# Six tiles wide at the start, squares on ScalarE, zero-padded rotary keys, and the samples' products in one run

## The chip, the core and the metric

The kernel runs on one core of a Trainium2 chip. TensorE (PE) multiplies matrices, VectorE (DVE) and ScalarE (ACT) work element by element, GpSimd (POOL) does the same more slowly and issues transfers, and SyncE (SP) issues most of the transfers. Each engine works through its own instructions in order and waits on semaphores for the others. The metric is the device time of one launch in microseconds (us), median of three runs.

## What is computed

One step of one layer for 256 prompt tokens and 8 samples of 16 tokens each, so 384 columns of tokens (`T`), with a model width of 2048. The layer has a group of eight latent-attention heads, a group of four gated-linear-attention heads (keys of 128, values of 256), an output projection, a gated feed-forward part and an embedding gate. What matters here:

```python
a = rms_norm(h, g_pre_mix)
z = a @ w_in                      # q-latent, kv-latent, rotary key, GLA q, k, v, gate, output gate
# latent attention, per head
s = einsum('bqhc,bkc->bhqk', q_lat, ckv) + einsum('bqhr,bkr->bhqk', q_rope, kr)   # kr: 64 wide, one for all heads
# gated linear attention of the samples: one block of 16 tokens, state S0 (8 samples, 4 heads, 128, 256)
attn = einsum('bthd,btshd,bshd->bhts', qf, decay, kf)
o  = einsum('bhts,bshv->bthv', attn, vf) + einsum('bthd,bhdv->bthv', qf * exp(b), S0)
S1 = exp(b_last)[..., None] * S0 + einsum('bshd,bshv->bhdv', kf * exp(b_last[:, None] - b), vf)
```

All inputs and outputs are float32.

## The kernel before, in words

**Products.** Large products run at float32 accuracy out of three faster ones. A weight chunk arrives in `raw`; ACT casts it to a high part `wh` (L89) and DVE subtracts to get the low part `wl` (L90); activations are split the same way (`ah`, `al`, L113 and L114). `mm3` (L98 to L101) then issues three matmuls per tile: high by high, high by low, low by high, over 384 columns. In names of the trace the tile written stands left of the arrow. Small products are plain float32 matmuls, of which one shows as two records in the trace.

**The start.** Eight matmuls on zeros (`warm`, L122) come first. `gemm_group` computes the four tiles of the GLA queries (`qg`), for 16 k-steps of 128 rows, with 12 matmuls per step in the first steps. For each k-step `load_x` loads a slice of x (SP, L274), makes its high and low parts, squares it on POOL (L280 for the first, L283 for the other 15) and adds the square to `ssx` on DVE (L284). `ssx` gives the norm's factor `rx` through `col_sums` (tile `sx`, L147). The banks are evicted with `rx` (L309). After it come the `misc` tile (rotary key and gate, L99 to L101 on 80 rows), four key tiles `kg` one by one (`win_tile`), then the statistic `pr` (L336).

**The samples' stage.** It is interleaved with the products `ckv` and `uq`, whose matmuls fill PE. For each half of the samples (four samples): the keys are transposed (`pk`, L574) and placed (`ks`, L577 and L579), the values are moved by POOL's transfers (`vs`, L585). Two output banks are opened by a matmul of zeros over the whole bank (L591), the scores' products of 32 columns add to them (L595, 16 per half, into four groups of 32 rows), and then, head by head, two states are loaded (POOL, L603) and four products of 16 columns with them (L606). The new states take a product (`pst`, L612), an update on DVE (L615) and a store (POOL, L617). Tiles come from a ring of ten buffers with the tag `tmp`. POOL also subtracts two low parts of the mixer's input there (`mixl`, L109).

**The prompt's scores.** The attention loop goes over four pairs of heads. For each head and each block of queries (128 and 256 columns wide) one product with the latent keys (nope, L703, contraction 128) is followed by one with the rotary keys (L704): the two heads of a pair lie in rows 0 to 63 and 64 to 127 of `cqn`, and the rotary keys stand twice in `krd`, so the contraction is over 64 rows.

**What sets the order.** The program is written in stages, and a scheduler that simulates the engines puts each engine's instructions in order by priorities; `tc.high_priority` moves loads and splits ahead, `tc.issue_after` holds a transfer behind an instruction. The order is fixed when the program is built.

Of the kernel before, what the change touches and what calls it, by code (L numbers as in the profile page):

```python
# [56 lines left out]
def layer(ctx: ExitStack, tc: tile.TileContext, I, O):  # L57
# [12 lines left out]
    PIECES = ((1, 1, 1, 1), (2, 2), (2, 2), (4,))  # L70
# [53 lines left out]
    with tc.high_priority(offset=2 * PRIO):  # L124
        sp.dma_start(out=gains, in_=I["gains"])
# [52 lines left out]
    def gemm_wide(srcs, a, name):  # L178

        banks = [bank(f"{name}{n}", "g" if n < 4 else "s") for n in range(WIDE)]  # L180
        cols = WIDE * P
        for c in range(NK // 2):
            pieces = (1, 1) if c == 0 else (2,)
            raw = stream.tile([P, 2048], F32, name="raw", tag="raw")
            k0 = 2 * c
            for n in pieces:
                with tc.high_priority(offset=PRIO):
                    at_k = (k0 - 2 * c) * cols
                    piece = raw[:, at_k:at_k + n * cols]
                    sp.dma_start(out=piece, in_=srcs[c][:, at_k:at_k + n * cols])  # L190
                    subs = split(piece, n * cols, cols)
                for k in range(n):
                    for m in range(WIDE):
                        mm3(banks[m][:, :T], at(subs[k], slice(None), slice(m * P, m * P + P)), a(k0 + k),
                            k0 + k == 0, k0 + k == NK - 1)
                k0 += n
        return [b[:, :T] for b in banks]

    def gemm_group(srcs, a, name, before=None):

        banks = [bank(f"{name}{n}") for n in range(4)]
        k0 = 0
        for c in range(4):
            pieces = PIECES[c] if before else PIECES[0 if c == 0 else 3]
            if len(pieces) > 1:
                raw = stream.tile([P, 2048], F32, name="raw", tag="raw")
            for i, n in enumerate(pieces):
                if before:
                    before(k0, n)
                if len(pieces) > 1:  # L210
                    with tc.high_priority(offset=PRIO):
                        at_k = sum(pieces[:i])
                        piece = raw[:, at_k * 512:(at_k + n) * 512]
                        sp.dma_start(out=piece, in_=srcs[c][:, at_k * 512:(at_k + n) * 512])
                        subs = split(piece, n * 512)
                else:
                    subs = weights(srcs[c])
                order = [(k, m) for k in range(n) for m in range(4)]
                if c == 3:
                    order = [(k, m) for m in range(4) for k in range(n)]  # L220
                for k, m in order:
                    w = subs[k // 2]
                    col = (k % 2) * 512 + m * P
                    kk = k0 + k
                    mm3(banks[m][:, :T], at(w, slice(None), slice(col, col + P)), a(kk), kk == 0, kk == NK - 1)
                k0 += n
        return [b[:, :T] for b in banks]
# [64 lines left out]
    win = iter(range(29))  # L292
# [35 lines left out]
    for h in range(GH):  # L328
        ps = win_tile("kg")
        for c in range(3):  # L330
            sl = slice(c * P, (c + 1) * P)
            dve.tensor_tensor(out=kg[c][:, h, :], in0=ps[:, sl], in1=rx[:, sl], op=ALU.mult)
# [216 lines left out]
    with tc.high_priority(offset=AHEAD):  # L549
# [12 lines left out]
        zero = gla.tile([P, 512], F32R, name="zero", tag="tmp", bufs=NTMP)  # L562
        pool.memset(zero.bitcast(F32), 0.0)
        for half in range(2):
# [23 lines left out]

            po = [bank("o", "s") for _ in range(2)]
            for o in po:  # L590
                pe.matmul(o, lhsT=zero[:, :P], rhs=zero, start=True, stop=False)  # L591
            for h in range(GH):
                for j in range(4):
                    col = h * P + (4 * half + j) * LB
                    pe.matmul(po[h // 2][32 * j:32 * j + 32, h % 2 * DV:(h % 2 + 1) * DV], lhsT=ats[:, col:col + 32],  # L595
                              rhs=vt[:, 2, h * DV:(h + 1) * DV], start=False, stop=False)
            for h in range(GH):
                s0 = []
                for i in range(2):
                    b = 4 * half + 2 * i  # L600
                    s0.append(gla.tile([P, 2, DV], F32, name="s0", tag="tmp", bufs=NTMP))
                    with tc.high_priority(offset=400), tc.issue_after(last_sq[-1].ins):
                        pool.dma_start(out=s0[i], in_=I["state"][b:b + 2, h].rearrange("b d v -> d b v"))  # L603
                for j in range(4):
                    b = 4 * half + j
                    pe.matmul(po[h // 2][32 * j:32 * j + LB, h % 2 * DV:(h % 2 + 1) * DV],  # L606
                              lhsT=qe[:, h, b * LB:(b + 1) * LB], rhs=s0[j // 2][:, j % 2], start=False, stop=h % 2 == 1)
                for i in range(2):
# [5 lines left out]
                    for e in range(2):  # L614
                        dve.scalar_tensor_tensor(out=s0[i][:, e], in0=s0[i][:, e], scalar=ebs[:, h, b + e:b + e + 1],  # L615
                                                 in1=pst[:, e * DV:(e + 1) * DV], op0=ALU.mult, op1=ALU.add)
                    pool.dma_start(out=O["gla_s"][b:b + 2, h].rearrange("b d v -> d b v"), in_=s0[i])  # L617
# [49 lines left out]

    smask = cst[:, C_SM:C_SM + 3 * P]
    for hp in range(4):
# [28 lines left out]
        for n in range(2):  # L698
            h = 2 * hp + n
            rows = slice(64 * n, 64 * n + 64)  # L700
# [432 lines left out]
```

## Time and profile before

| what | value |
|---|---|
| three runs | 1902.71, 1901.04, 1902.37 us |
| median | 1902.37 us |
| the profiled execution, its own time | 1902.81 us |
| its span, first to last instruction | 1901.0 us |
| busy: PE | 1883.6 us (99%) |
| busy: DVE, ACT, POOL | 974.7, 690.2, 80.4 us |
| mean granted clock of TensorE | 0.998 |

The span is 1.8 us shorter than that execution's own time; this lies around it. PE is the busiest engine by far, and the chain of work that ended last runs along it for 78% of the span. Busy means that an instruction is under way: it doesn't tell whether that instruction runs at its best rate. This is read from the distance between the starts of neighbouring matmuls in the timeline.

### The profile page before, as it was taken

What the parts mean: (1) busy time and instruction counts of PE and PEld (TensorE: products, weight loads), DVE (VectorE), ACT (ScalarE), POOL (GpSimd) and SP (SyncE); (2) the same over time, 40 slices, a digit from 0 to 9 for tenths busy, and PEclk for the clock granted to TensorE, in tenths of its full rate; (3) what the DMA queues carried; (4) which work ended last, traced back from release to release, by engine and by line L of the source; (5) the groups of instructions that cost most, each with busy time, mean ns of one, the idle gap of its engine ahead of it and who ended that gap; (6) DMA issues with size and microseconds to landing.
All of it is one profiled execution on the core that took longest, in us unless ns stands there. A gap on an engine that the chain in (4) does not pass through costs nothing.

```text
span 1901.0 us, 24107 instructions
## 1 busy us (share of the span) xinstructions
PE 1883.6 (99%) x10026; PEld 1709.8 (90%) x10026; DVE 974.7 (51%) x1368; ACT 690.2 (36%) x1044; POOL 80.4 (4%) x122
## 2 busy tenths in 40 slices
PE   8999999999999999999999999999999999999998
PEld 8989998788999988889988998899888988899998
DVE  7445756754233395445334643554355435456753
ACT  4344545643233453333333222322232222325432
POOL 4000002411000000000000000000000000000010
PEclk9999999999999999999999999999999999999999
DMA  6333325635743333343333333333333333334351
GB/s 239 136 110 112 112 89 176 213 138 204 258 169 133 130 122 133 111 136 130 133 133 123 122 133 133 129 118 130 133 133 111 133 133 133 111 111 147 128 177 67
DMA packets 43311, 262.53 MB, mean 138 GB/s; under 512 B 5441, under 2 KB 6481, under 8 KB 17090
## 3 DMA queue, kind: packets, MB, share of 16 engines
q1 hardware_dynamic: 36018, 233.76, 35.7%
q0 software_dynamic: 7184, 27.23, 4.1%
q8 instruction: 78, 1.28, 0.3%
q14 instruction: 31, 0.25, 0.0%
HBM read 251.17 MB, written 8.75 MB: 137 GB/s over the span
## 4 chain that ended last, share of the span: by engine, by line
PE 78%; DVE 1%; ACT 0%; issue 0%; DVEq 0%; ACTq 0%
PE gu L896 12%; PE gu L897 12%; PE gu L895 12%; PE dn L101 6%; PE dn L100 6%; PE dn L99 6%; PE mix L101 2%; PE pg L99 2%; PE pg L101 2%; PE pg L100 2%; PE mix L99 2%; PE mix L100 2%; PE psc L774 2%; PE pol L800 2%; PE ps L704 0%; DVE zT L957 0%
## 5 line engine op out<-in xcount | busy, mean ns | idle before, releaser
L90 DVE TENSOR_TENSOR wl<-raw,wh 128x1024 fp32r<-128x1024 f32 (+2 forms) x426 | 512.0, 1203 | 652.5 <-ACT wh L89 651.5
L89 ACT CAST wh<-raw 128x1024 fp32r<-128x1024 f32 (+2 forms) x426 | 435.8, 1023 | 980.5 <-PE gu L897 448.8
L896 PE MATMUL gu<-wl,fh 128*128 128x512 f32 x1056 | 411.5, 390 | 0.1
L897 PE MATMUL gu<-wh,fl 128*128 128x512 f32 x1056 | 409.2, 389 | 0.0
L895 PE MATMUL gu<-wh,fh 128*128 128x512 f32 x1056 | 406.9, 389 | 0.1
L896 PEld LDWEIGHTS gu<-wl,fh 128*128 128x128 f32 x1056 | 198.2, 188 | 42.7 <-DVE wl L90 1.7
L895 PEld LDWEIGHTS gu<-wh,fh 128*128 128x128 f32 x1056 | 198.2, 188 | 41.3 <-ACT fh L113 0.4
L897 PEld LDWEIGHTS gu<-wh,fl 128*128 128x128 f32 x1056 | 198.2, 188 | 41.0
L99 PE MATMUL dn<-sh,wh 128*128 128x384 f32 x704 | 235.1, 334 | 0.0
L100 PE MATMUL dn<-sl,wh 128*128 128x384 f32 x704 | 235.1, 334 | 0.0
L101 PE MATMUL dn<-sh,wl 128*128 128x384 f32 x704 | 234.7, 335 | 0.0
L101 PEld LDWEIGHTS dn<-sh,wl 128*128 128x128 f32 x704 | 132.0, 188 | 1.3 <-DVE wl L90 1.3
L99 PEld LDWEIGHTS dn<-sh,wh 128*128 128x128 f32 x704 | 132.1, 188 | 0.2
L100 PEld LDWEIGHTS dn<-sl,wh 128*128 128x128 f32 x704 | 132.1, 188 | 0.2
L957 DVE STREAM_TRANSPOSE zT<-z 32x384 f32<-32x384 f32 x176 | 100.3, 570 | 2.8
L984 DVE TENSOR_TENSOR acc<-acc,dn 128x384 f32<-128x384 f32 x80 | 44.3, 553 | 99.2 <-PE dn L101 98.8
L99 PE MATMUL mix<-mixh,wh 128*128 128x384 f32 x256 | 85.6, 334 | 0.0
L101 PE MATMUL pg<-h2h,wl 128*128 128x384 f32 x256 | 85.5, 334 | 0.0
L100 PE MATMUL pg<-h2l,wh 128*128 128x384 f32 x256 | 85.5, 334 | 0.0
L100 PE MATMUL mix<-mixl,wh 128*128 128x384 f32 x256 | 85.5, 334 | 0.0
L101 PE MATMUL mix<-mixh,wl 128*128 128x384 f32 x256 | 85.5, 334 | 0.0
L99 PE MATMUL pg<-h2h,wh 128*128 128x384 f32 x256 | 82.6, 334 | 0.0
(358 smaller groups left out, 2417.9 us busy)
## 6 DMA issues: line engine op xcount, KB each, us to landing
raw<-in_wgu SPq DMA_DIRECT2D x87, 1024.0 KB, 4.8
raw<-in_wd SPq DMA_DIRECT2D x40, 1024.0 KB, 4.8
raw<-in_win SPq DMA_DIRECT2D x20, 1024.0 KB, 4.9
raw<-in_wout SPq DMA_DIRECT2D x16, 1024.0 KB, 4.8
raw<-in_wpg SPq DMA_DIRECT2D x10, 1024.0 KB, 4.8
raw<-in_wvg SPq DMA_DIRECT2D x8, 1024.0 KB, 4.9
keys<-in_ckT POOLq DMA_DIRECT2D x8, 1024.0 KB, 5.6
raw<-in_ck SPq DMA_DIRECT2D x8, 1024.0 KB, 5.0
```

Of the source, the lines that this page charges most:

```text
L89: act.copy(out=h[:, :n], in_=raw[:, c:c + n])
L90: dve.tensor_tensor(out=l[:, :n], in0=raw[:, c:c + n], in1=h.bitcast(F32)[:, :n], op=ALU.subtract)
L99: pe.matmul(out, lhsT=w[0], rhs=a[0], start=start, stop=False)
L100: pe.matmul(out, lhsT=w[0], rhs=a[1], start=False, stop=False)
L101: pe.matmul(out, lhsT=w[1], rhs=a[0], start=False, stop=stop)
L774: pe.matmul(ps[:, :HK], lhsT=q.rearrange("p h t -> p (h t)"), rhs=keys[:, j, i * HK:(i + 1) * HK], start=j == 0, stop=j == 4)
L800: pe.matmul(o, lhsT=vals[:, k, j * P:(j + 1) * P], rhs=pT[:, k], start=k == 0, stop=False)
L895: pe.matmul(out[c], lhsT=ah, rhs=w[0], start=k == 0, stop=False)
L896: pe.matmul(out[c], lhsT=ah, rhs=w[1], start=False, stop=False)
L897: pe.matmul(out[c], lhsT=al, rhs=w[0], start=False, stop=k == NK - 1)
L957: dve.transpose(out=dst[cols, :, :, rows], in_=src[rows, :, :, cols])
L984: dve.tensor_tensor(out=acc[:, n], in0=acc[:, n], in1=ps, op=ALU.add)
```

## The change

Four parts:

- The first group is six tiles wide: `gemm_wide` computes four `qg` and two `kg` tiles together (tile `qk`), from a weight laid out by k-steps (`wqk`), 18 matmuls per step. The first weight piece is loaded as 256 and 512 columns. `gemm_group` and `PIECES` go. The squares of x are ScalarE activations, the gains are loaded from ACT's queue, and the constants and the statistic come at k = 14.
- The samples' scores are copied to a zeroed tile `aw` of 128 columns per head; four full products per half open the banks, and the zero products and the 32-wide products go.
- All eight states of a half are loaded first; the products with them then stand in one run, from the last head to the first; the updates follow in that order.
- The rotary keys are copied to `krz`, once with rows 64 to 127 zero and once with rows 0 to 63 zero, so the rotary product contracts over 128 rows of `cqn`.

```diff
-    def gemm_wide(srcs, a, name):
+    def gemm_wide(srcs, a, name, before=None):
...
-            pieces = (1, 1) if c == 0 else (2,)
+            pieces = (1, 1) if c < (2 if before else 1) else (2,)
...
+                if before:
+                    before(k0, n)
...
+                    parts = ((0, 2 * P), (2 * P, cols)) if before and k0 == 0 else ((0, n * cols),)
+                    for lo, hi in parts:
+                        piece = raw[:, at_k + lo:at_k + hi]
+                        sp.dma_start(out=piece, in_=srcs[c][:, at_k + lo:at_k + hi])
+                        subs += [(w, lo % cols) for w in split(piece, hi - lo, cols)]
...
-        sp.dma_start(out=gains, in_=I["gains"])
+        act.dma_start(out=gains, in_=I["gains"])
...
-                pool.tensor_tensor(out=ssx, in0=xk, in1=xk, op=ALU.mult)
+                act.activation(out=ssx, in_=xk, func=AF.Square)
...
-                last_sq.append(pool.tensor_tensor(out=sq, in0=xk, in1=xk, op=ALU.mult))
+                last_sq.append(act.activation(out=sq, in_=xk, func=AF.Square))
...
-        if k0 == 12:
+        if k0 == 14:
...
-    for h, ps in enumerate(gemm_group(I["wqg"], a, "qg", load_x)):
+    for h, ps in enumerate(gemm_wide(I["wqk"], a, "qk", load_x)):
+        if h >= GH:
+            keys(h - GH, ps)
+            continue
...
-            for o in po:
-                pe.matmul(o, lhsT=zero[:, :P], rhs=zero, start=True, stop=False)
+            aw = tmp(gla)
+            pool.memset(aw, 0.0)
+            act.copy(out=aw.rearrange("p (h j t) -> p h j t", h=GH, j=4)[:, :, :, :LB],
+                     in_=at_[2][:, :, 64 * half:64 * half + 64].rearrange("p h (j t) -> p h j t", j=4))
             for h in range(GH):
-                for j in range(4):
-                    col = h * P + (4 * half + j) * LB
-                    pe.matmul(po[h // 2][32 * j:32 * j + 32, h % 2 * DV:(h % 2 + 1) * DV], lhsT=ats[:, col:col + 32],
-                              rhs=vt[:, 2, h * DV:(h + 1) * DV], start=False, stop=False)
+                pe.matmul(po[h // 2][:, h % 2 * DV:(h % 2 + 1) * DV], lhsT=aw[:, h * P:(h + 1) * P],
+                          rhs=vt[:, 2, h * DV:(h + 1) * DV], start=h % 2 == 0, stop=False)
...
+            for h in reversed(range(GH)):
+                for j in (3, 2, 1, 0):
                     b = 4 * half + j
                     pe.matmul(po[h // 2][32 * j:32 * j + LB, h % 2 * DV:(h % 2 + 1) * DV],
-                              lhsT=qe[:, h, b * LB:(b + 1) * LB], rhs=s0[j // 2][:, j % 2], start=False, stop=h % 2 == 1)
+                              lhsT=qe[:, h, b * LB:(b + 1) * LB], rhs=s0[h][j // 2][:, j % 2], start=False, stop=h % 2 == 0)
...
+    krz = of[:, 8:10]
+    pool.memset(krz, 0.0)
+    for e in range(2):
+        rows = slice(64 * e, 64 * e + 64)
+        act.copy(out=krz[rows, e], in_=krd[rows, :TP])
...
-                pe.matmul(o, lhsT=cqn[rows, hp, qt], rhs=krd[rows, kt], start=False, stop=True)
+                pe.matmul(o, lhsT=cqn[:, hp, qt], rhs=krz[:, n, kt], start=False, stop=True)
```

How the order of instructions moves. The first place is ACT at the start. `ah` is the high part of a slice of x, `wh` that of a weight piece. Before:

```order
L116 ACT_TABLE_LOAD
L113 ACTIVATE ah_99<-x,gains 128x384
L89 CAST wh<-raw 128x512
L113 ACTIVATE ah_99<-x,gains 128x384
L89 CAST wh<-raw 128x512
```

Now, where `ssx<-x` and `ev<-x` are squares:

```order
L124 DMA gains<-in_gains 128x74
L115 ACT_TABLE_LOAD
L257 ACTIVATE ssx<-x 128x384
L112 ACTIVATE ah_99<-x,gains 128x384
L88 CAST wh<-raw 128x256
L88 CAST wh<-raw 128x512
L112 ACTIVATE ah_99<-x,gains 128x384
L260 ACTIVATE ev<-x 128x384
L88 CAST wh<-raw 128x768
```

The gains' issue and the squares have come to ACT, and the casts are of 256 and 512 columns at first, then of 768.

The second place is PE in the first half of the samples' stage. `o` is the samples' output bank, `s_` with a number a state tile, `ckv` the product between which it stands. Before:

```order
L101 MATMUL ckv<-ah_101,wl 128x384
L591 MATMUL o<-zero 128x512
L595 MATMUL o<-vt,atts 32x256 x3
L591 MATMUL o<-zero 128x512
L595 MATMUL o<-vt,atts 32x256 x13
L606 MATMUL o<-s_2929,qeb 16x256 x2
L606 MATMUL o<-s_2931,qeb 16x256 x2
L606 MATMUL o<-s_2949,qeb 16x256 x2
L606 MATMUL o<-s_2951,qeb 16x256 x2
L606 MATMUL o<-s_2969,qeb 16x256 x2
L606 MATMUL o<-s_2971,qeb 16x256 x2
L99 MATMUL ckv<-ah_101,wh 128x384
```

Now, where `tmp` in `o<-vt,tmp` is the padded score tile `aw`:

```order
L98 MATMUL ckv<-ah_101,wh 128x384
L590 MATMUL o<-s_2937,qeb 16x256
L576 MATMUL o<-vt,tmp 128x256 x2
L590 MATMUL o<-s_2937,qeb 16x256
L590 MATMUL o<-s_2935,qeb 16x256 x2
L590 MATMUL o<-s_2933,qeb 16x256 x2
L590 MATMUL o<-s_2931,qeb 16x256 x2
L99 MATMUL ckv<-al_102,wh 128x384
```

The run is now of eight state products and starts with a later load; the other eight of the half (two heads) stand together 36 products further on, where two pairs stood alone before.

The third place is POOL in the second half of that stage, where loads of states, stores of new states and the two subtractions `mixl` share one queue. Now:

```order
L584 DMA s_3080<-in_state 128x2x256
L584 DMA s_3082<-in_state 128x2x256
L602 DMA out_gla_s<-s_2937 128x2x256
L602 DMA out_gla_s<-s_2931 128x2x256
L108 ISA
L108 TENSOR_TENSOR mixl_3282<-og,mixh_3281 128x8x128
L602 DMA out_gla_s<-s_2933 128x2x256
L584 DMA s_3084<-in_state 128x2x256
L584 DMA s_3086<-in_state 128x2x256
L108 TENSOR_TENSOR mixl_3282<-og,mixh_3281 128x8x128
```

Before, a load stood ahead of each of the two subtractions and the third and fourth load behind both; now two loads stand ahead, two between them, and the instruction `ISA` (POOL's library) has come from the first square to here. On PE at the prompt's scores of the first pair of heads, `ps` before:

```order
L703 MATMUL ps<-kv,qn 128x128
L704 MATMUL ps<-krd,cqn 128x128
L703 MATMUL ps<-kv,qn 128x256
L704 MATMUL ps<-krd,cqn 128x256
L703 MATMUL ps<-kv,qn 128x128
L704 MATMUL ps<-krd,cqn 128x128
L703 MATMUL ps<-kv,qn 128x256
L704 MATMUL ps<-krd,cqn 128x256
```

Now, behind 40 products since the two nope products of 128 columns (`of` holds the padded keys):

```order
L695 MATMUL ps<-of,cqn 128x128
L694 MATMUL ps<-kv,qn 128x256
L695 MATMUL ps<-of,cqn 128x256
L695 MATMUL ps<-of,cqn 128x128
L694 MATMUL ps<-kv,qn 128x256
L695 MATMUL ps<-of,cqn 128x256
```

The rotary product takes the padded keys, and in this pair the first two nope products stand ahead of the rest.

## Rows read from the trace of the kernel before

**Rows 1.** The page's first part: busy time, share and instructions of each engine.

```profile
PE 1883.6 (99%) x10026; PEld 1709.8 (90%) x10026; DVE 974.7 (51%) x1368; ACT 690.2 (36%) x1044; POOL 80.4 (4%) x122
```

**Rows 2.** Waits of PE: engine and line, waited for, total us, times, longest.

```profile
PE qg L101 <- DVE wl L90: 2.6, 2, 2.3
PE pk L574 <- DVE s L615: 2.4, 1, 2.4
PE pv L692 <- ACT kv L685: 1.5, 1, 1.5
```

**Rows 3.** Timeline of PE, start: start us, us, operation, count, idle before and releaser.

```profile
6.28 0.69 PE L99 MATMUL qg<-ah,wh 128*128 128x384 f32 x1 [1.04 <-ACT wh L89]
...
10.29 1.02 PE L99 MATMUL qg<-ah,wh 128*128 128x384 f32 x3
...
37.11 0.44 PE L101 MATMUL qg<-ah,wl 128*128 128x384 f32 x1 [2.34 <-DVE wl L90]
...
47.81 0.34 PE L99 MATMUL misc<-ah,wh 128*80 128x384 f32 x1
...
56.18 0.33 PE L99 MATMUL kg<-ah,wh 128*128 128x384 f32 x1
```

**Rows 4.** Windows: us, busy of PE, PEld, DVE, ACT, POOL, clock, DMA share, GB/s.

```profile
20.00:30.00 10.00, 9.89 (x57) 9.57 (x57) 10.00 (x13) 4.15 (x6) 5.75 (x4) 1.00 0.77 302
```

**Rows 5.** Groups by line and shape: count, busy us, mean ns, idle before.

```profile
L114 DVE SCALAR_TENSOR_TENSOR al<-x,gains,ah 128x384 fp32r<-128x384 f32 x16 | 13.7, 878 | 2.6 <-ACT ah L113 2.6
...
L114 DVE SCALAR_TENSOR_TENSOR fl<-hh,gains,fh 128x384 fp32r<-128x384 f32 x16 | 9.8, 614 | 0.2 <-ACT fh L113 0.2
...
L90 DVE TENSOR_TENSOR wl<-raw,wh 128x768 fp32r<-128x768 f32 x16 | 15.3, 956 | 10.1 <-ACT wh L89 10.0
...
L89 ACT CAST wh<-raw 128x768 fp32r<-128x768 f32 x16 | 13.4, 836 | 17.8 <-PE pg L100 14.1 <-issue 3.3 <-PE ple L100 0.4
```

**Rows 6.** Timeline of PE in the samples' stage, both halves.

```profile
308.16 0.40 PE L591 MATMUL o<-zero 128*128 128x512 f32 x1
...
311.02 1.67 PE L606 MATMUL o<-s,qeb 128*16 128x256 f32 x21
312.62 0.45 PE L99 MATMUL ckv<-ah,wh 128*128 128x384 f32 x1
...
316.89 0.34 PE L99 MATMUL ckv<-ah,wh 128*128 128x384 f32 x1
...
317.98 0.34 PE L101 MATMUL ckv<-ah,wl 128*128 128x384 f32 x1
...
348.08 0.50 PE L591 MATMUL o<-zero 128*128 128x512 f32 x1
...
351.79 0.44 PE L101 MATMUL uq<-cqhl,wl 128*128 128x384 f32 x1
```

**Rows 7.** Timeline of PE: full-array float32 products, and the first pair's scores.

```profile
278.60 1.89 PE L485 MATMUL pst<-vt,tmp 128*128 128x256 f32 x8
280.32 1.03 PE L470 MATMUL o<-vt,attp 128*128 128x256 f32 x4
...
387.72 0.39 PE L703 MATMUL ps<-kv,qn 128*128 128x128 f32 x2
...
391.79 0.39 PE L99 MATMUL pkn<-ckhl,wh 128*128 128x256 f32 x1
...
403.55 0.39 PE L725 MATMUL po<-pT,kv 128*128 128x128 f32 x2
...
404.67 0.39 PE L728 MATMUL po<-pT,kv 128*128 128x128 f32 x2
```

**Rows 8.** Timelines of DVE and POOL in the samples' stage.

```profile
338.12 7.48 DVE L90 TENSOR_TENSOR wl<-raw,wh 128x1024 fp32r<-128x1024 f32 x1
...
338.30 2.41 POOL L109 TENSOR_TENSOR mixl<-og,mixh 128x1024 fp32r<-128x1024 f32 x1
```

**Rows 9.** Timeline of POOL at the start.

```profile
3.75 0.82 POOL L280 TENSOR_TENSOR ssx<-x 128x384 f32<-128x384 f32 x1 [3.30 <-DMA x<-in_xT]
```

More of the change, by code (lines that the diff above doesn't have):

```diff
@@ L192, in gemm_wide @@
                 for k in range(n):
                     for m in range(WIDE):
-                        mm3(banks[m][:, :T], at(subs[k], slice(None), slice(m * P, m * P + P)), a(k0 + k),
+                        w, lo = subs[k if n == len(subs) else int(m >= 2)]
+                        col = m * P - lo
+                        mm3(banks[m][:, :T], at(w, slice(None), slice(col, col + P)), a(k0 + k),
                             k0 + k == 0, k0 + k == NK - 1)
-                k0 += n
-        return [b[:, :T] for b in banks]
@@ L199, in gemm_group @@
[L199 to L225, printed above, removed]
@@ L290, in load_x @@
                 rstd(rx, col_sums(ssx, T, "sx"), DM)
-    win = iter(range(29))
+    win = iter(range(26))
     def win_tile(name, m=P, order=None):
@@ L303, in win_tile, with keys @@
         return ps
-    for h, ps in enumerate(gemm_group(I["wqg"], a, "qg", load_x)):
+    def keys(h, ps):
+        for c in range(3):
+            sl = slice(c * P, (c + 1) * P)
+            dve.tensor_tensor(out=kg[c][:, h, :], in0=ps[:, sl], in1=rx[:, sl], op=ALU.mult)
+    for h, ps in enumerate(gemm_wide(I["wqk"], a, "qk", load_x)):
+        if h >= GH:
+            keys(h - GH, ps)
+            continue
         for c in range(3):
@@ L326, in layer @@
     pool.dma_start(out=O["krT"], in_=krd[0:64])
[L328 to L332, printed above, removed]
+    for h in range(WIDE - GH, GH):
+        keys(h, win_tile("kg"))
     pr = bank("pr", "s")
@@ L561, in layer @@
             dve.tensor_tensor(out=vl[:, half], in0=vt[:, 2, half], in1=vh.bitcast(F32), op=ALU.subtract)
-        zero = gla.tile([P, 512], F32R, name="zero", tag="tmp", bufs=NTMP)
-        pool.memset(zero.bitcast(F32), 0.0)
         for half in range(2):
@@ L589, in layer @@
             po = [bank("o", "s") for _ in range(2)]
-            for o in po:
-                pe.matmul(o, lhsT=zero[:, :P], rhs=zero, start=True, stop=False)
+            aw = tmp(gla)
+            pool.memset(aw, 0.0)
+            act.copy(out=aw.rearrange("p (h j t) -> p h j t", h=GH, j=4)[:, :, :, :LB],
+                     in_=at_[2][:, :, 64 * half:64 * half + 64].rearrange("p h (j t) -> p h j t", j=4))
             for h in range(GH):
-                for j in range(4):
-                    col = h * P + (4 * half + j) * LB
-                    pe.matmul(po[h // 2][32 * j:32 * j + 32, h % 2 * DV:(h % 2 + 1) * DV], lhsT=ats[:, col:col + 32],
-                              rhs=vt[:, 2, h * DV:(h + 1) * DV], start=False, stop=False)
+                pe.matmul(po[h // 2][:, h % 2 * DV:(h % 2 + 1) * DV], lhsT=aw[:, h * P:(h + 1) * P],
+                          rhs=vt[:, 2, h * DV:(h + 1) * DV], start=h % 2 == 0, stop=False)
+            s0 = [[None, None] for _ in range(GH)]
             for h in range(GH):
-                s0 = []
                 for i in range(2):
                     b = 4 * half + 2 * i
-                    s0.append(gla.tile([P, 2, DV], F32, name="s0", tag="tmp", bufs=NTMP))
+                    s0[h][i] = gla.tile([P, 2, DV], F32, name="s0", tag="tmp", bufs=NTMP)
                     with tc.high_priority(offset=400), tc.issue_after(last_sq[-1].ins):
-                        pool.dma_start(out=s0[i], in_=I["state"][b:b + 2, h].rearrange("b d v -> d b v"))
-                for j in range(4):
+                        pool.dma_start(out=s0[h][i], in_=I["state"][b:b + 2, h].rearrange("b d v -> d b v"))
+            for h in reversed(range(GH)):
+                for j in (3, 2, 1, 0):
                     b = 4 * half + j
                     pe.matmul(po[h // 2][32 * j:32 * j + LB, h % 2 * DV:(h % 2 + 1) * DV],
-                              lhsT=qe[:, h, b * LB:(b + 1) * LB], rhs=s0[j // 2][:, j % 2], start=False, stop=h % 2 == 1)
+                              lhsT=qe[:, h, b * LB:(b + 1) * LB], rhs=s0[h][j // 2][:, j % 2], start=False, stop=h % 2 == 0)
+            for h in reversed(range(GH)):
                 for i in range(2):
@@ L614, in layer @@
                     for e in range(2):
-                        dve.scalar_tensor_tensor(out=s0[i][:, e], in0=s0[i][:, e], scalar=ebs[:, h, b + e:b + e + 1],
+                        dve.scalar_tensor_tensor(out=s0[h][i][:, e], in0=s0[h][i][:, e], scalar=ebs[:, h, b + e:b + e + 1],
                                                  in1=pst[:, e * DV:(e + 1) * DV], op0=ALU.mult, op1=ALU.add)
-                    pool.dma_start(out=O["gla_s"][b:b + 2, h].rearrange("b d v -> d b v"), in_=s0[i])
+                    pool.dma_start(out=O["gla_s"][b:b + 2, h].rearrange("b d v -> d b v"), in_=s0[h][i])
             toks = slice(TP + 64 * half, TP + 64 * half + 64)
@@ L699, in layer @@
             h = 2 * hp + n
-            rows = slice(64 * n, 64 * n + 64)
             ps = bank("ps")
```

9 lines of the change are left out of this document (3 added, 6 removed).

## The prediction

> **What bounds the kernel now.** The page's engine table comes first: TensorE (PE) is busy in nearly all of the span [rows 1], so a gain must come out of PE's own time: its waits, matmuls that take longer than they need, or matmuls that go. The waits of PE, sorted by their sum [rows 2], name two in the samples' stage (2.4 and 1.5 us) and one at the start. The timeline of PE at the start [rows 3] shows the rest: the warm-up matmuls end at 5.24 (6.28 less an idle 1.04), the 192 products of the first group start at 6.28, wait 2.34 at 37.11 for VectorE's (DVE) low part, and end at 47.81. Undisturbed, 48 misc products take 56.18 - 47.81 = 8.37, or 0.174 each, the 2.4 GHz level; the first twelve, 6.28 to 10.29, take 0.334 each, near the 1.2 GHz level. DVE is busy for the whole of the window from 20 to 30 us [rows 4]: there it is DVE, and not PE, that sets the pace. Why, [rows 5] tell: the scaled low part of x takes 878 ns on average while GpSimd (POOL) squares x, and 614 ns for the same shape later. [rows 6] and [rows 7] show PE busy at a bad rate: the samples' scores and state products, and the alternation of nope and rotary products. An fp32 product shows as two records of the trace, so x2 is one instruction.
>
> **Part 1, the start.** Removed from POOL: 16 squares; from DVE: their disturbance; from the load queue (SP): the gains, ahead of x. Added to ScalarE (ACT): 16 squares and the gains' issue, ahead of its table load. The first weights come as 256 + 512 columns, so the first cast has half the data to wait for. Per k-step PE now has 18 products instead of 12: 18 x 0.174 = 3.13 us. DVE needs for a k-step one low part of x (0.614), one sum (of the same size, so taken as 0.61) and one low part of 768 columns (0.956): 2.2 us. ACT needs a cast (0.836) and two operations of 384 columns, taken as 0.61 each by the nearest DVE row: 2.1 us [rows 5]. Both lie under PE's 3.13, so the wait at 37.11 goes and PE is next late in the first k-step alone. The sum: from 5.24 to 47.81 are 42.57 us; 192 x 0.174 = 33.4 is work and the statistic's product about 0.7; the loss is 8.5. After the change a first k-step near the low clock costs again 12 x (0.334 - 0.174) = 1.9, and with an idle start of 0 to 0.3 the loss is about 2.1. The gain is 6.4. Bounds: if the clock rises earlier, as there is no idle between warm-up and work, the loss is 0.5 and the gain 8.0; if a wait of the old size (2.3) stays, the gain is 4.1. I take 6.4, since the row at 6.28 to 10.29 is the same work. Two key tiles move into the first group: the same products, no cost. The constants are issued at k = 14 instead of 12 and are needed only after the misc tile, 8.4 us of PE later, so this costs nothing. The six banks are read out under those same 48 products; were that cover gone, misc would wait for a free bank, at most some tenths.
>
> **Part 2, the samples' stage.** Before, the blocks of zero products, 32-wide score products and state products take 312.62 - 308.16 = 4.5 us in half 0 and 351.79 - 348.08 = 3.7 in half 1. A pair of state products alone between weight products costs 317.98 - 316.89 - 2 x 0.174 = 0.74 [rows 6]; such pairs stand alone 8 times, 2 in half 0 and 6 in half 1, 5.9 in all. With an estimate of 0.4 for entering and leaving the two blocks, which their starts don't hold, this is 14.5. In a run the state records follow each other at (312.62 - 311.02)/21 = 0.076 us, so the four records of a pair are 0.30, and entering and leaving a run costs 0.44. After: 8 full products of 128x256 at 1.72/4 = 0.43 [rows 7] are 3.4, some 0.6 for the places where they stand alone between weight products (0.2 each, as the alternation in part 3), 64 state records are 4.9, and five runs (four, one of them broken up by score products) 5 x 0.44 = 2.2; 11.1 in all. The gain is 3.4. Bounds: 4.5 if the entry is cheaper in long runs; 2.5 if one run more is broken up. The padded score tile needs a POOL memset and an ACT copy, off the path unless a wait for the tile's buffer makes it late: that is the first rival.
>
> **Part 3, the rotary scores.** Before, one head pair's 8 products take 391.79 - 387.72 = 4.07 us; four pairs alike. Their sizes are half 128 and half 256 columns. Full-array products one after the other take (404.67 - 403.55)/5 = 0.224 for 128 columns and 0.43 for 256 [rows 7], so 4 x 0.224 + 4 x 0.43 + 0.1 = 2.7. The rest, 1.36 of 4.07, belongs to the change of tile shape at each of the 7 steps, about 0.19 each. With keys padded by zeros to 128 rows every product is a full-array one: 4 x 1.36 = 5.4. The first pair stands in two pieces in the new program (its two first nope products ahead, then 40 others), which costs one more entry, 0.2. The gain is 5.2; bounds 4.6 and 5.5. The keys' padding is one memset and two copies; 40 products stand between the first nope product and the first rotary one, so they hide it.
> What a 64-row product costs is thus a matter of its neighbours. The Trainium skill's page TensorEngine Tiling (Array Packing), section Tiling Modes, says that a change of tiling mode drains TensorE, and its section Performance Considerations advises 64-row tiles for a contraction of 64, since such tiles can work side by side. By the first rule the 5.2 stands; by the second padding throws away half an array and would gain nothing. Here no two 64-row products of different rows stand next to each other, and the trace agrees with the first.
>
> **Part 4, the waits of the samples' stage.** Before: 2.4 + 1.5 = 3.9 [rows 2]. The 2.4 come from one DVE subtraction of 1024 columns that lasts 7.48 us beside a POOL subtraction (2.41, a second like it follows) [rows 8], where 768 columns take 0.956 elsewhere, so some 1.3 would be expected. In the new program the two POOL subtractions stand behind other loads and stores, and so fall on other DVE work: the wait can vanish (+3.9 with the other one), or come back at another place with some more (-1.0). I take +1.8, near the middle, since the collision moves and doesn't disappear.
> The Trainium skill's page SBUF — State Buffer, section Who interferes with whom, calls the shared port pair a lock which one instruction holds for its whole length, the other blocking; by that a DVE operation would lose at most one POOL operation's length, about 2.4, and the sum would gain some 2 more. The trace shows a loss of over 6 in one instruction, so the measurement decides.
> POOL also loads its instruction library before its first tensor operation. That was hidden in the 3.30 us idle ahead of the first square [rows 9]; now it stands before the first POOL subtraction of the samples' stage. Its price lies between 0 and these 3.3 us, on POOL's queue, and reaches PE only through the state loads behind it. I take 0 to 1, inside the -1.0 above.
>
> **Sum.** 6.4 + 3.4 + 5.2 + 1.8 = 16.8 from the profiled execution's own 1902.81 gives 1886.0. The median of the runs is 0.4 lower than that execution, so the forecast is 1885.6.
>
> **Rivals.**
> *New waits in the samples' stage.* The state products now run in eights and PE works in order, so the first product of a run stops all until its load has landed; the stores that free buffers come later than before. For it: half 1's third and fourth load stand on POOL right behind a subtraction and a store that waits for DVE. Against: before, no product waits for a state load, and weight products stand ahead of the runs. Price: another delay like the 7.48 row (6.2 too long) in place of the 1.8 gain: 1885.6 + 1.8 + 6.2 = 1893.6; a lesser one gives 1889.
> *The start is bound by data or stays cold.* If the transfers of the first steps, now 50% more per step, leave PE waiting 2 to 4 us, or if the low clock holds for two steps, the gain is 2.5 to 4: 1888 to 1889.5.
> *Padding gives nothing.* If a full-array rotary product takes what the 64-row one with its change took, part 3 is 0: 1890.8. Against: [rows 7] has full-array products at the short pitch.
> *Slower.* One mechanism: the chain of POOL's queue in half 1. A store waits for a delayed DVE operation (7.48), the next load waits behind it and behind two POOL subtractions (2 x 2.41), and PE stands before the run: 12.3 us. Once, this gives 1897.9, still faster; at both runs of half 1 it gives 24.6 and 1910.2. It decides from 16.8 us of such waiting on. Against: the two chains would have to be one after the other, while the same POOL work serves both runs.
> *The change doesn't do what it says.* The program order shows that runs stand together, except that one product of half 0 is parted from its run. Were a scheduler's order to break each run in two, 4 x 0.44 = 1.8 would go: 1887.4.
>
> **How the numbers follow.** Forecast 0.60 (its own bounds: best 8.0 + 4.5 + 5.5 + 3.9 = 21.9, 1880.5; worst 4.1 + 2.5 + 4.6 - 1.0 = 10.2, 1892.2, both from the median); new waits 0.16; the start 0.12; padding 0.05; broken runs 0.04; slower 0.03. The range is 1879.5 to 1892.5, which holds the forecast's bounds, the start, the padding and the lesser waits, and leaves out 0.15 or so above. A measurement of this kernel tells 0.2%, or 3.8 us, from no change: faster by more 0.93, within 0.04 (waits that eat 13 us or more), slower 0.03.
>
> **What would show it.** In the profile after: the first product right at the end of the warm-up, near 5.3; no wait of PE before 60; DVE well under full in the 10 to 30 windows; misc at 57 to 59 (with 96 products more before it, 10.5 + 15 x 3.13 + 0.7). Score pairs of 2.7 us. State runs of 16 records in 1.2 us (16 x 0.076). The waits of PE in the samples' stage at 2 to 3 us in sum. It is wrong if a wait for a state load or for a score tile of over 4 us stands there, if misc starts after 61, or if score pairs take over 3.5.

## The result, and the profile after

Four runs of the changed kernel beside four of before gave a median of 1883.22 us against 1902.54; the ratio is 0.9894, interval 0.9877 to 0.9910. The profiled execution among them ran at a granted clock of 0.654 and took 2668.71 us, so nothing of it is read here; the other three have a median of 1882.67. The kernel was run again (e1 below) for a profile: 1880.32 against 1902.06, ratio 0.9893, interval 0.9877 to 0.9908. The change takes some 20 us away, 1.1%. All that follows reads the profile of that second run, whose own time is 1880.47 with a span of 1878.7.

The page's first part, and PE's waits in sorted order (engine and line, waited for, us, times, longest):

```profile
PE 1867.4 (99%) x9974; PEld 1707.4 (91%) x9974; DVE 964.4 (51%) x1371; ACT 698.0 (37%) x1067; POOL 62.2 (3%) x108
```

```profile
PE pkn L98 <- DVE cqn L619: 1.9, 1, 1.9
PE warm L121 <- DVE warm L118: 1.5, 1, 1.5
PE pol L791 <- DVE pT L785: 1.3, 2, 0.7
PE qk L98 <- ACT wh L88: 0.5, 1, 0.5
```

Against [rows 1], PE's busy time has fallen by 16.2 us and its idle time by about 6. Against [rows 2], the three waits there are gone and one of 1.9 has come, for DVE's rotary addition.

Where the 22 us between the two profiled executions went is read from the first matmul of a tile in each timeline of PE:

| stretch of PE's work | before | changed | difference |
|---|---|---|---|
| to the last `pz` product (start) | 110.36 | 102.61 | -7.75 |
| first `ckv` to first `pkn` (samples, rotation) | 90.72 | 84.24 | -6.48 |
| first `pkn` to first `pql` (prompt's attention) | 46.49 | 39.57 | -6.92 |
| first `pql` to first `mix` | 96.72 | 96.08 | -0.64 |

The last two rows belong together, since the order at the border between them differs: before, six `po` products of the prompt (1.35 us) stand behind the first `pql`, and in the changed kernel ahead of it. Together the two rows are -7.56. The first of these products before:

```profile
427.63 0.39 PE L725 MATMUL po<-pT,kv 128*128 128x128 f32 x2
```

Timeline of PE at the start (start us, us, operation, count, idle before):

```profile
1.46 3.78 PE L121 MATMUL warm<-warm 128*128 128x512 f32 x8 [1.46 <-DVE warm L118]
5.03 0.74 PE L98 MATMUL qk<-ah,wh 128*128 128x384 f32 x2
5.61 0.52 PE L99 MATMUL qk<-al,wh 128*128 128x384 f32 x2
6.62 0.44 PE L98 MATMUL qk<-ah,wh 128*128 128x384 f32 x1 [0.50 <-ACT wh L88]
6.90 0.34 PE L99 MATMUL qk<-al,wh 128*128 128x384 f32 x1
7.08 0.35 PE L98 MATMUL qk<-ah,wh 128*128 128x384 f32 x1
```

Only the first four products run at about 0.3 us; from 6.90 on the distance is 0.18, the 2.4 GHz level, where [rows 3] have the low level up to 10.29. PE was busy from 1.46 to 6.1 without a pause this time; before, it paused 1.04 at 5.24 (e2 below shows that the pause alone doesn't decide when the clock rises). After 6.62 no wait follows in the first 60 us. DVE's groups in the same time (count, busy us, mean ns), and the window of [rows 4] in the changed kernel:

```profile
L113 DVE SCALAR_TENSOR_TENSOR al<-x,gains,ah 128x384 fp32r<-128x384 f32 x16 | 9.2, 614 | 2.7 <-ACT ah L112 2.7
L261 DVE TENSOR_TENSOR ssx<-ssx,ev 128x384 f32<-128x384 f32 x15 | 8.3, 554 | 0.3
```

```profile
20.00:30.00 10.00, 10.00 (x60) 10.00 (x59) 9.79 (x17) 7.72 (x15) 0.00 (x0) 1.00 0.83 306
```

The low part of x has gone from the 878 ns of [rows 5] to the 614 it has elsewhere. But DVE is still busy for 9.79 of these ten us, where the prediction looked for a DVE well under full: it works ahead, and PE waits for nothing. So a full DVE, before or now, doesn't say that DVE sets the pace; PE's waits do. Timeline of PE in the samples' stage, a run of eight state products and a pair of padded score products:

```profile
299.03 0.34 PE L99 MATMUL ckv<-al,wh 128*128 128x384 f32 x1
299.20 1.02 PE L576 MATMUL o<-vt,tmp 128*128 128x256 f32 x4
299.88 0.52 PE L100 MATMUL ckv<-ah,wl 128*128 128x384 f32 x1
300.24 0.34 PE L98 MATMUL ckv<-ah,wh 128*128 128x384 f32 x1
...
310.30 0.34 PE L98 MATMUL ckv<-ah,wh 128*128 128x384 f32 x1
310.57 1.06 PE L590 MATMUL o<-s,qeb 128*16 128x256 f32 x16
311.56 0.44 PE L99 MATMUL ckv<-al,wh 128*128 128x384 f32 x1
311.84 0.34 PE L100 MATMUL ckv<-ah,wl 128*128 128x384 f32 x1
```

The run costs 311.84 - 310.30 - 2 x 0.174 = 1.19 us, the score pair 300.24 - 299.03 - 2 x 0.174 = 0.86, or 0.43 for one product. And one head pair's scores:

```profile
388.72 0.38 PE L694 MATMUL ps<-kv,qn 128*128 128x128 f32 x2
...
390.91 0.59 PE L695 MATMUL ps<-of,cqn 128*128 128x256 f32 x2
391.15 0.47 PE L98 MATMUL pkn<-ckhl,wh 128*128 128x256 f32 x1
391.46 0.28 PE L99 MATMUL pkn<-ckhl,wh 128*128 128x256 f32 x1
```

The eight products take 2.43 us to the start of the next product, where [rows 7] have 4.07. The way out costs more now: counted to the second next product it is 2.74, against 4.29 before (the next starts 0.22 after 391.79).

### The profile page after: what moved, and what is told of

It is laid out like the page before. It is cut to its first block, busy times and chain, and to the rows that moved or that the text cites. A ratio compares the mean times of both kernels' runs of the same rounds, so it can differ in the third digit from the quotient of the medians.

```text
span 2666.9 us, 24010 instructions
## 1 busy us (share of the span) xinstructions
PE 2658.2 (100%) x9974; PEld 1992.0 (75%) x9974; DVE 968.9 (36%) x1371; ACT 699.0 (26%) x1067; POOL 61.8 (2%) x108
## 4 chain that ended last, share of the span: by engine, by line
PE 99%; DVE 0%; DMA 0%; issue 0%; ACT 0%; SPq 0%; DVEq 0%
PE gu L887 13%; PE gu L888 13%; PE gu L886 13%; PE dn L98 6%; PE dn L100 6%; PE dn L99 6%; PE mix L99 2%; PE pg L98 2%; PE pg L99 2%; PE mix L100 2%; PE mix L98 2%; PE pg L100 2%; PE psc L765 2%; PE pol L791 2%; PE v L387 1%; PE v L386 1%
## 5 line engine op out<-in xcount | busy, mean ns | idle before, releaser
L89 DVE TENSOR_TENSOR wl<-raw,wh 128x1024 fp32r<-128x1024 f32 (+3 forms) x429 | 506.5, 1181 | 1159.2 <-ACT wh L88 1158.0
L88 ACT CAST wh<-raw 128x1024 fp32r<-128x1024 f32 (+3 forms) x429 | 434.8, 1014 | 1651.0 <-PE gu L888 762.2
L887 PE MATMUL gu<-wl,fh 128*128 128x512 f32 x1056 | 535.9, 507 | 0.0
L888 PE MATMUL gu<-wh,fl 128*128 128x512 f32 x1056 | 533.8, 507 | 0.0
L886 PE MATMUL gu<-wh,fh 128*128 128x512 f32 x1056 | 530.6, 507 | 0.0
L98 PE MATMUL dn<-sh,wh 128*128 128x384 f32 x704 | 298.7, 425 | 0.0
L99 PE MATMUL dn<-sl,wh 128*128 128x384 f32 x704 | 298.7, 424 | 0.0
L100 PE MATMUL dn<-sh,wl 128*128 128x384 f32 x704 | 297.7, 424 | 0.0
L98 PE MATMUL mix<-mixh,wh 128*128 128x384 f32 x256 | 108.8, 425 | 0.0
L100 PE MATMUL mix<-mixh,wl 128*128 128x384 f32 x256 | 108.8, 425 | 0.0
```

The lines of the kernel that those rows point to most:

```text
L88: act.copy(out=h[:, :n], in_=raw[:, c:c + n])
L89: dve.tensor_tensor(out=l[:, :n], in0=raw[:, c:c + n], in1=h.bitcast(F32)[:, :n], op=ALU.subtract)
L98: pe.matmul(out, lhsT=w[0], rhs=a[0], start=start, stop=False)
L99: pe.matmul(out, lhsT=w[0], rhs=a[1], start=False, stop=False)
L100: pe.matmul(out, lhsT=w[1], rhs=a[0], start=False, stop=stop)
L886: pe.matmul(out[c], lhsT=ah, rhs=w[0], start=k == 0, stop=False)
```

## The experiments

Each ratio is that of the run's times to those of the kernel before on the same chip, with its 95% interval. Three reasons stood for the start (the squares on POOL, the width, the cold clock), two for the rotary products (change of tile shape, or work side by side), and two for the waits (POOL beside DVE, or DVE's own load).

**e1, the changed kernel again.**

> The changed kernel once more, for a profile at the full clock and the split of its gain. Forecast's steps: 1881 to 1885 us; the first product at 5.2 to 5.6, no wait of PE before 60 us, misc at 57 to 59, a score pair (8 products) 2.7 us, state runs of 16 records 1.2 us, waits of PE between 300 and 400 us of 2 to 3 us in sum (before 4.6). If the 2.5 us by which the measured 1883.2 lies under the forecast 1885.6 come from the start (clock up earlier), misc starts at 55.5 to 57; if they come from the samples' waits, their sum is near 0.

1880.32 us, 0.9893 (0.9877 to 0.9908). `misc` starts at 57.21 and the only wait between 300 and 400 us is the 1.9 one. `misc` gives no verdict between the two reasons, since the statistic and a part of `pr` stand ahead of it; the timeline above does: the clock was up early. Of the signs that the prediction named, the first product (5.03), `misc`, the run of 1.19 and, nearly, the sum of the waits (1.9) hold; the 0.50 us wait ahead of 6.62 and the busy DVE do not.

**e2, the whole start undone.** `gemm_group`, squares on POOL and gains on SP as before, samples and keys as changed.

> The start as before (four query tiles, squares on POOL, gains on SP), the other three parts as changed. Theory: the start alone is worth 6.4 us, so 1889 to 1890.5. If the clock rises earlier without the idle, it is worth 8: 1891 to 1892. If the changed start is bound by its data, it is worth 2.5 to 4: 1885.5 to 1887.5.

1889.28 us, 0.9938 (0.9926 to 0.9950): 9.0 above e1, inside the theory's times and more than its 6.4. The profiled execution is the slowest of its six (1892.27). Timeline of PE at its start:

```profile
5.93 0.45 PE L99 MATMUL qg<-ah,wh 128*128 128x384 f32 x1 [0.87 <-ACT wh L89]
6.21 0.34 PE L100 MATMUL qg<-al,wh 128*128 128x384 f32 x1
```

The products are at the 2.4 GHz level from 6.21 on, behind a pause of 0.87 us, so what this start lacks is not an early clock. PE waits 4.3 us in four places for DVE's low part, and behind these waits the granted clock falls further than before (the column ahead of the DMA share), first this run, then the kernel before:

```profile
40.00:50.00 10.00, 10.00 (x42) 9.34 (x42) 3.24 (x11) 2.06 (x4) 0.00 (x0) 0.72 0.30 105
```

```profile
40.00:50.00 10.00, 10.00 (x53) 9.03 (x52) 5.00 (x15) 2.89 (x4) 0.00 (x0) 0.91 0.40 121
```

The last `pz` stands at 112.30, 1.9 later than in the profile of before, which has the same code there. So a start with these waits also varies from run to run, by the waits and by the clock behind them.

**e3, the samples' stage undone.**

> The samples' stage as before (zero products, 32-wide score products, states in pairs), the other parts as changed. Theory: 3.4 for the products and 1.8 for the waits, together 1887.5 to 1889. If all waits of that stage left with the change: 1890 to 1891. If new waits have eaten the gain: 1883 to 1885.

1890.59 us, 0.9944 (0.9932 to 0.9956): 10.3 above e1, at the upper case. The waits of before are back (2.4 for `pk`, 1.5 for `pv`), the 1.9 is gone. In this profile the granted clock is 0.93 and 0.90 in the two windows of ten us from 330 to 350, around and behind the 2.4 wait, by an estimate 1.7 us of work lost; in the kernel before it stays at 1.00 behind the same wait. So a part of the 10.3 is the clock.

**e4, the padded keys undone.**

> The rotary products over 64 rows as before, the other parts as changed. Theory (each change of tile shape costs 0.19 us): +5.2, so 1887.5 to 1889, with score pairs of 4.07 us again. Rival (a padded product takes what the 64-row one took): no difference, 1882 to 1884.

1887.41 us, 0.9926 (0.9914 to 0.9937): 7.1 above e1. A pair of heads takes 4.07 again (4.30 to the second next product). The rival is out. The three single undoings add up to 26.4, more than the whole change gives: each also moves the order of the rest, so one part alone is priced better by the table above.

**e5, the squares back on POOL, the group still six wide.**

```diff
-                act.activation(out=ssx, in_=xk, func=AF.Square)
+                pool.tensor_tensor(out=ssx, in0=xk, in1=xk, op=ALU.mult)
```

> The changed kernel with the squares of x back on POOL; the group stays six tiles wide. Theory, width alone is enough: DVE needs per k-step 0.88 + 0.80 (its slowed operations) and about 1.1 for the low part of 768 columns, 2.8 us, under PE's 3.13, so only the first steps lose: 1880.5 to 1882. Rival, the squares' place is what counts: waits for the low part come back with 2 to 4 us: 1882.5 to 1885.

1887.43 us, 0.9928 (0.9915 to 0.9942): 7.1 more than e1, beyond even the rival's price. Windows of this kernel (PE, PEld, DVE, ACT and POOL busy, clock, DMA share, GB/s), and DVE's groups:

```profile
20.00:30.00 10.00, 7.71 (x35) 7.39 (x34) 10.00 (x14) 3.07 (x6) 5.04 (x5) 0.83 0.69 254
```

```profile
L89 DVE TENSOR_TENSOR wl<-raw,wh 128x768 fp32r<-128x768 f32 x15 | 15.5, 1034 | 10.0 <-ACT wh L88 10.0
L113 DVE SCALAR_TENSOR_TENSOR al<-x,gains,ah 128x384 fp32r<-128x384 f32 x16 | 14.0, 893 | 2.2 <-ACT ah L112 2.2
```

DVE's low part of x is back at 893 ns; PE waits 2.7 us, and the granted clock falls to 0.83 in this window, as it fell to 0.92 and 0.91 in the two windows from 30 to 50 us around and behind the [rows 3] wait. The last `pz` stands at 108.77, 6.2 later than in e1, of which the listed waits are less than half. The theory summed DVE's mean times of a step to 2.8 us, under PE's 3.13, and fell all the same. DVE is full from 10 to 40 us and at 34% in the ten us behind, while PE works on the group until 62.8: as in e1, it does the work of later steps early, and the low part that PE waits for stands behind some of it. A sum per step doesn't hold that order. This is read from the windows and was not tried by itself.

**e6, four tiles wide, but squares and gains on ACT.**

> The four query tiles alone as the first group, as before, but with the squares on ACT and the gains on ACT's queue; samples and keys as changed. Theory, DVE undisturbed is enough: DVE needs per k-step 0.61 + 0.55 + 0.68 = 1.84 us, PE 12 x 0.174 = 2.09, so no wait but at the first steps: 1880 to 1882. Rival, the width is needed: the start stays as with all of it undone, 1886 to 1890. Together with the runs that undo all of the start and the squares alone this makes a square of four.

1880.73 us, 0.9892 (0.9878 to 0.9905): the same as e1. Timeline of PE at its start:

```profile
5.50 0.96 PE L99 MATMUL qg<-ah,wh 128*128 128x384 f32 x4 [0.26 <-ACT wh L89]
6.30 0.85 PE L100 MATMUL qg<-al,wh 128*128 128x384 f32 x4
```

With ACT's squares the start is as good narrow as wide: the last `pz` stands at 102.19. The square of four: squares on ACT 1880.3 (wide) and 1880.7 (narrow), on POOL 1887.4 and 1889.3. With the squares on ACT, where both have the gains on ACT's queue, the width is worth nothing that can be measured. The pair on POOL differs in the gains' queue as well (e2 has SP's), so its 1.9 is not the width alone.

**e7, no padding, the two heads' rotary products next to each other.**

> No padded keys; the rotary products over 64 rows of the two heads stand next to each other (2 nope, 2 rotary of 128 columns, then 2 and 2 of 256): 3 changes of tile shape per pair of heads instead of 7. Theory, each change costs 0.19 us and a 64-row product otherwise what a full one does: 2.7 + 3 x 0.19 = 3.2 us per pair, 1882 to 1883. Rival of the notes, products in different rows work side by side: half of the rotary time goes, 2.6 or less per pair, 1878 to 1880.5. If the 64-row product itself is slow: about 4 per pair, 1886 to 1888.

1881.83 us, 0.9897 (0.9883 to 0.9910). Timeline of PE, one pair of heads:

```profile
375.33 0.61 PE L686 MATMUL ps<-kv,qn 128*128 128x128 f32 x4
375.87 0.49 PE L689 MATMUL ps<-krd,cqn 64*128 64x128 f32 x4
376.29 1.13 PE L686 MATMUL ps<-kv,qn 128*128 128x256 f32 x4
377.35 0.70 PE L689 MATMUL ps<-krd,cqn 64*128 64x256 f32 x4
377.99 0.39 PE L98 MATMUL pkn<-ckhl,wh 128*128 128x256 f32 x1
```

Two 64-row products (x4 records) take 0.42 us from 375.87 on. That is what one alone took in the kernel before, in the timeline of [rows 7]:

```profile
388.03 0.49 PE L704 MATMUL ps<-krd,cqn 64*128 64x128 f32 x2
388.45 0.70 PE L703 MATMUL ps<-kv,qn 128*128 128x256 f32 x2
```

They do run side by side, and the pair takes 2.66. The median isn't under e1's. The profile, of the slowest of the four executions (1884.28), has one more wait, 1.9 for the values' transfer (`pst`), and a granted clock of 0.90 and 0.93 in the two windows from 310 to 330 around and behind it, by an estimate another 1.7 us.

**e8, the rotary swap in the other ring of banks.**

```diff
-        psw = bank("psw")[:, :T]
+        psw = bank("psw", "s")[:, :T]
```

> The changed kernel with the rotary swap's product (psw) in the other ring of PSUM banks, so that the keys' product pkn doesn't stand behind DVE's last use of it. Theory, the new wait of 1.9 us (pkn for DVE's rotary addition) is one for a bank: it goes, 1878 to 1879, and no wait of its size takes its place. Rival, DVE is the pace there: the same wait comes at another product, 1880 to 1881.

1879.38 us, 0.9881 (0.9868 to 0.9895). The wait of `pkn` is gone from the list; 0.5 for `vs` has come. So it was one for a bank that DVE had not freed yet. The gain in time, about 1, is less than the interval's half width (0.13%, 2.5 us), and the trace carries the verdict.

**e9, the kernel before with the squares on ACT and nothing else.**

> The kernel before with one edit: the 16 squares of x are ScalarE activations instead of POOL products. Nothing else is changed; the gains stay on SP's queue. Theory, POOL's squares slow DVE and DVE sets the pace of the start: the waits of 2.3 go and DVE's low part of x falls from 878 to about 614 ns; 7 to 8.5 us, 1893 to 1895. Rival, the other edits of the start carry a good part of it: 1896 to 1899.

1895.65 us against 1900.88, 0.9968 (0.9956 to 0.9981): 5 to 6 us, between the two. Timeline of PE:

```profile
5.87 0.69 PE L99 MATMUL qg<-ah,wh 128*128 128x384 f32 x1 [0.63 <-ACT wh L89]
...
10.20 0.48 PE L100 MATMUL qg<-al,wh 128*128 128x384 f32 x1
10.51 0.33 PE L99 MATMUL qg<-ah,wh 128*128 128x384 f32 x1
```

The low part of x is down to 615 ns and no wait for `wl` is left, but with 0.63 idle at 5.24 the distance stays at 0.32 until 10.4. e6, with the gains off SP's queue and 0.26 idle, is at the full level by 6.3 and has its last `pz` at 102.19 instead of 104.59. So the squares give the larger part. The rest is 2.4: 0.37 for the earlier first product and, by the distances, about 2 for the products at the 1.2 GHz level. e2 had the high level early with the gains on SP's queue, so whether moving the gains brings it is not shown; the gains alone were not tried.

**e10, the kernel before with the mixer's subtraction on DVE.**

```diff
-        to_hl(mix(...), og[...], pool if c < 2 else dve)
+        to_hl(mix(...), og[...], dve)
```

> The kernel before with one edit: the two subtractions for the mixer's input (mixl) in the samples' stage run on DVE instead of POOL. Theory, the 7.48 us of one DVE subtraction came from the POOL subtractions beside it: no DVE operation of 1024 columns there lasts over 1.5 us, the wait of 2.4 goes, 1899 to 1900.5 (DVE has 2.4 us more of its own work). Rival, that DVE operation was long for another reason: 1901 to 1903 and the wait stays.

1897.92 us, 0.9982 (0.9974 to 0.9991): 3.0 less than before, under the theory's 1899. The second of the two POOL subtractions before, and the timeline of DVE in this run where [rows 8] have 7.48:

```profile
342.11 2.40 POOL L109 TENSOR_TENSOR mixl<-og,mixh 128x1024 fp32r<-128x1024 f32 x1
```

```profile
337.12 1.22 DVE L90 TENSOR_TENSOR wl<-raw,wh 128x1024 fp32r<-128x1024 f32 x1
338.25 1.23 DVE L109 TENSOR_TENSOR mixl<-og,mixh 128x1024 fp32r<-128x1024 f32 x1
```

The same subtraction takes 1.22, the mixer's subtractions 1.23 each; the wait of 2.4 is gone and that of 1.5 down to 0.6: DVE does more and is done sooner.

**e11, all four nope products, then all four rotary ones over 64 rows.**

> No padded keys; per pair of heads all four nope products, then all four rotary products over 64 rows, the two heads next to each other (one accumulation group per bank). Theory, products in different rows run side by side and a change of tile shape costs some 0.1 to 0.2 us: 1.31 for nope, 0.65 for two times two rotary products, 0.3 for the change in and out, 2.25 per pair against 2.65 with padded keys, so 1.6 us under the changed kernel: 1878 to 1880. Rival, the side by side of the last run was worth only what its changes cost and grouping brings nothing more: 2.65 per pair, 1880 to 1882.

1881.17 us, 0.9894 (0.9881 to 0.9908). Timeline of PE, one pair of heads, and a wait from its list:

```profile
374.42 1.48 PE L687 MATMUL ps<-kv,qn 128*128 128x128 f32 x8
375.82 0.93 PE L691 MATMUL ps<-krd,cqn 64*128 64x128 f32 x8
376.68 0.39 PE L98 MATMUL pkn<-ckhl,wh 128*128 128x256 f32 x1
```

```profile
PE o L590 <- DMA s<-in_state: 1.3, 1, 1.3
```

2.26 us a pair, as the theory said, the four rotary products 0.86. But a state run waits 1.3 for its load here, and the time isn't lower than e1's. To the second next product the pair is 2.48 against e1's 2.74, so only 1.0 of the 1.6 was there to gain. The time lies in the rival's range, the pair in the theory's.

**e12, e8 and e11 together.**

> The changed kernel with the rotary products four together over 64 rows and the rotary swap's product in the other ring of banks. Theory: 1.6 and 1.0 us under the changed kernel, 1877 to 1879. Rival, the two meet on the same banks and one gain goes: 1879 to 1881.

1876.75 us, 0.9873 (0.9859 to 0.9886), just under the theory's 1877. The lowest of all, with no wait over 0.7 behind the warm-up's. Its interval overlaps that of e1 a little; the two were on different chips.

## Why the prediction was right, point by point

The forecast was 1885.6 in a range of 1879.5 to 1892.5; 1883.2 and 1880.3 lie inside, the second at the sum of all best bounds (1880.5). The mechanisms held, and all four sizes were too small: 22.3 us lie between the two profiles, where the sum had 16.8. That the range held is in part luck, since two terms left their own bounds.

- **The start**, 6.4 forecast, 7.75 in the trace. The cause was right: POOL's squares slow DVE, and PE waits for DVE's low part (e5, e9). The term mis-sized is the cold first step: 1.9 was taken over from [rows 3], and four products at the low level came. The bound of 8.0 had this case, but its reason, no idle between warm-up and work, is not shown: e2 had the pause and the early clock. The lower bound of 4.1 priced a wait of 2.3 by its own length. e5 has that wait, and by its last `pz` its start gains 1.6; the clock of 0.83 behind it alone is 1.7 us by an estimate (0.17 of ten us). That 18 products per step give DVE room was no part of the gain (e6).
- **The samples' products**, 3.4 forecast, over its bound of 4.5. The table's -6.48 holds the waits (2.4 and 0.7 gone, 1.9 come, -1.2), so -5.3 is the products; the granted clock is 1.00 in this stage in both profiles. Two terms were too dear: a run of 16 records was taken at 16 x 0.076 + 0.44 = 1.65 and takes 1.19; and nothing is added to 0.43 for a full product between weight products, where 0.2 was. The 0.44 had been read from pairs standing alone, and doesn't carry over to a long run.
- **The rotary products**, 5.2 forecast, 6.1 in the last two rows of the table (7.56 less the wait of 1.5), over its bound of 5.5. A pair, counted to the second next product, went from 4.29 to 2.74, or 1.55 less where the sum had 1.36, and the extra 0.2 of the first pair doesn't show. The price of the alternation was right in kind (e4). The reason was half of it: the rival's premise, that 64-row products of different rows work side by side, which the Trainium skill's page TensorEngine Tiling (Array Packing) has in its section Tiling Modes, is true here as well (e7: two in the time of one). The alternating order of before used none of it.
- **The waits**, +1.8 forecast, 4.6 gone and 1.9 come, +2.7. The collision moved, as said. Timelines of DVE and POOL in the changed kernel:

```profile
328.97 2.98 DVE L89 TENSOR_TENSOR wl<-raw,wh 128x1024 fp32r<-128x1024 f32 x1
...
332.28 3.60 DVE L488 TENSOR_TENSOR ssl<-ssl,ev 128x384 f32<-128x384 f32 x1
```

```profile
328.49 2.39 POOL L108 TENSOR_TENSOR mixl<-og,mixh 128x1024 fp32r<-128x1024 f32 x1 [0.98 <-ACT mixh L107]
...
333.04 2.41 POOL L108 TENSOR_TENSOR mixl<-og,mixh 128x1024 fp32r<-128x1024 f32 x1
```

  DVE loses 2.98 - 1.23 = 1.75 and 3.60 - 0.55 = 3.05 us, but no product waits for these. By the rule of the page SBUF — State Buffer of the Trainium skill (section Who interferes with whom) neither should lose over 2.4; the first agrees, the second doesn't, nor did the 7.48. In all three the DVE operation ends at most its own undisturbed length behind the end of a POOL subtraction: at 345.60 behind 344.51, 331.95 behind 330.88, and 335.88 behind 335.45. Whether the transfers that POOL issued between (1.4 us in the 7.48) hold DVE as well is not shown: it issued one behind the subtraction that ended at 330.88, too, and there DVE was done in time. The forecast's new wait came elsewhere: the state updates, six of them at 358.35, stand before the rotation on DVE, and a bank comes free late:

```profile
358.35 2.43 DVE L600 SCALAR_TENSOR_TENSOR s<-s,ebs,pst 128x256 f32<-128x256 f32 x6
360.70 0.55 DVE L617 TENSOR_TENSOR psw<-psw,cst 128x384 f32<-128x384 f32 x1
```

- **The library's load** on POOL cost nothing that shows: no idle time over 1 us stands ahead of the first subtraction.
- Of the rivals, the wait for a state load came in e11 alone, with 1.3 us. The slower case was nowhere near.

What stays open: when the clock rises at the start and why it falls behind some waits of about 2 us and not behind others, the gains' share in the start, and why one DVE operation loses more than the POOL operation beside it lasts.

## What to carry to other kernels

An engine that looks lightly used can set the pace of another: look at the mean time of the same operation with and without GpSimd at work, and move the GpSimd part before widening or reordering anything. A full engine is not yet the pace: ask what the busiest engine waits for. A wait can cost more than its length, when the clock falls behind it. Matmuls of a part of the array are dear by the changes of shape around them, and cheap in groups; a long run costs less than pairs tell. When a stage gains on PE, the next wait is for a bank that a later-ordered engine still holds, and one line can move it.

## What the runs showed of the hardware that was not expected

Two 64-row products in different halves of the array took 0.42 us together (128 columns), as one did alone. A DVE subtraction of 1024 columns that takes 1.22 us took 7.48 beside two POOL subtractions of 2.4, with 1.4 us of transfers issued between them. At the start, in the kernel before, e9 and e10, with pauses of 1.04, 0.63 and 0.69 us behind the warm-up, the products stayed at the 1.2 GHz level until past 10 us; in e2, with a pause of 0.87, they were at 2.4 GHz by 6.21. In e1, e3 to e8, e11 and e12, whose first product came by 5.50, they were at that level by 6.3 to 7.7. So the length of the pause alone doesn't tell, and the windows' clock column shows 1.00 up to 10 us in all of these, so that only the distance of the products does. Behind a wait of PE of about 2 us the granted clock fell in some places, by an estimate from the windows 1.7 us of work (the kernel before at the start, e3, e5, e7 and e10), and stayed at 1.00 in others (the 2.4 in the samples' stage of the kernel before, the 1.9 in e1).
